# Expert blocks of a routed decoder layer: a second buffer for turned rows, a pause in queuing weight splits around turns, and one turn moved ahead of a product

## The chip, the cores and the metric

One core of a Trainium2 chip runs the whole program. The metric is the device time of one execution in microseconds (us), taken as the median of several executions; lower is better.

## The reference, cut to what matters

The layer mixes tokens (attention and a convolution), routes every token to 2 of 32 experts, and ends with a gated per-layer embedding. The change touches the experts alone:

```
def expert_block(args):               # 2048 tokens x 2 choices, grouped by expert, float32
    xb, e = args                      # xb: rows of one block of one expert, 1024 wide
    hdn = jax.nn.silu(xb @ w1[e]) * (xb @ w3[e])      # 512 wide
    return hdn @ w2[e]                                # 1024 wide
...
out = jnp.zeros((N + 1, D), ys.dtype).at[row_tok].add(ys * row_w[:, None])
```

## The kernel before

**Number format.** Every float32 factor is split into a high and a low part (`hi` is what the engine's reduced float32 keeps, `lo` the rest), and a product is made of three matmuls: hi by hi, hi by lo, lo by hi. A split is one copy on ScalarE (ACT, line 91, writes the high part) and one subtraction on VectorE (DVE, line 92, writes the low part).

**Slots and blocks.** The 32 experts are sorted by their number of tokens and put into 32 slots, 0 to 31. A slot holds one or two or three blocks. A full block has 128 rows; a small block (`few` in the code) has 64, and puts its high and low rows side by side in one operand, so that it needs two thirds of the matmuls. Slot 0 has two full blocks, slot 2 two full and one small, slots 4, 6 and 8 two full; slots 1, 3, 5, 7, 9, 11 and 13 one small; slots 10, 12, 14 and every even one to 30 a full and a small; slots 15, 17 and every odd one to 31 one full. Two blocks of a slot are worked as a pair, in turns; a single block is held over: its last products are made inside the next group.

**Weights.** A slot has 12 units of weights, each 128 x 1024 (512 KB): units 0 to 7 for the first two products, 8 to 11 for the last. "Unit 12.1" is unit 1 of slot 12 below. A unit is loaded to `eraw` (8 buffers, by SP's queue), and split to `ewh` on ACT and `ewl` on DVE (14 buffers of each).

**Steps of a block j.** X(j) turns the gathered rows by transposes on TensorE (PE, `tps<-cst,xs`) and splits them into `xt` (tag `xt` for a full block, `fx` for a small one). U(j,f,g) is a quarter of the first products (`ups`, f and g are 0 or 1; it reads units 4f+2g and 4f+2g+1); after g = 1 the block's hidden half f is made by `gated`: for a full block a SiLU on ACT and a multiplication on DVE (`hd`), for a small one a copy on ACT, an addition on DVE (`ft`), then these two. T(j,f) turns that half (`hps<-cst,hd`) and splits it into `hh`. DN(j,f,n) makes half n of the output from hidden half f (`yd`; units 8+2f and 9+2f). U of a full block is 12 matmuls of 512 columns, of a small one 8; DN 6 and 4. The transposes of X and T share two PSUM buffers (pool `et`).

**Order.** All engines run their instructions in the order in which `moe` writes them. The order of steps is written out by hand in the loop over groups. Between them the planner queues unit splits: `pe` and `dve` are clocks of its own that each step moves on, and `did`, called at the end of a step, pulls a unit as long as DVE's clock is at most 1.5 us ahead of PE's and a buffer will be free. U and DN pull what they need themselves, if it was not pulled yet, right before their own matmuls ("forced" below):

```
def U(j, f, g):
    while pulled <= 12 * j.e + 4 * f + 2 * g + 1:
        pull()
```

So the place of a split in the queues of ACT and DVE is fixed when the program is built, behind whatever was written before it, also if that waits for PE.

Of the kernel before, what the change touches and what calls it, by code (L numbers as in the profile page):

```python
# [10 lines left out]
F32R = mybir.dt.float32r  # L11
# [8 lines left out]
P = 128  # L20
# [3 lines left out]
NK = D // P  # L24
# [6 lines left out]
NE = 32  # L31
# [14 lines left out]
MOE_W = (8, 14)  # L46
# [15 lines left out]
SLACK = 1.5  # L62
# [20 lines left out]
class K:  # L83
# [808 lines left out]
    def pick(self):  # L892
# [34 lines left out]
        for g in range(4):  # L927
            nc.tensor.transpose(tp[:, g * P : (g + 1) * P], tab[:, g * P : (g + 1) * P], self.ident)
        turned = sp.tile([P, N], F32, name="turned", tag="hT")
        V.tensor_copy(turned, tp)  # L930
        dp = self.px.tile([P, N], F32, name="dps", tag="tps")
        for g in range(4):
# [39 lines left out]
    def moe(self):  # L972
# [11 lines left out]
        W, src, last = {}, [], {}  # L984
        self.last = W

        pe, dve, pulled = 0.0, 0.0, 0

        def pull():
            nonlocal pulled, dve  # L990
            e, c = pulled // 12, pulled % 12
            if c == 0:
                W[e] = []
                if e == NE:
                    src[:] = halves(A["wpp"]) + halves(A["pT"][1]) + [A["wpg"][c, i] for c in range(2) for i in range(4)]
                elif e:
                    i = nc.values_load(self.slots[0:1, 0, e : e + 1], engines=[ET.SP], min_val=0, max_val=NE - 1)
                    src[:] = [A["we"][bass.ds(i, 1), c] for c in range(12)]
                else:
                    src[:] = [A["we"][0, c] for c in range(12)]  # L1000
            W[e].append(self.unit(src[c], None, self.gathered if EARLY <= pulled < 12 else None))
            pulled += 1
            dve = max(dve, pe) + UNIT_US

        def did(us):

            nonlocal pe
            pe += us
            while dve <= pe + SLACK and pulled < 12 * NE + 12 and (pulled < MOE_W[1] or pulled - MOE_W[1] in last):
                pull()  # L1010

        def small(us):
            nonlocal dve
            dve = max(dve, pe) + us
# [9 lines left out]
        def rows(k):  # L1024
            if k < len(jobs) and jobs[k].x is None:
                j = jobs[k]
                j.x = self.xp.tile([P, D], F32, name="xs", tag="xs")[j.R]
                self.gather(col(self.idx, j.e, j.b)[j.R], j.x)

        def X(j):  # L1030
            if j is None or j.done:
                return
            j.done = True
            j.xt = self.turned(j.x, j.few)
            rows(j.k + 2)
            small(0.64 if j.few else 1.28)
            did(0.5 if j.few else 0.87)
# [4 lines that stand above are left out]
            w = W[j.e]  # L1042
            if g == 0:
                j.u[f] = self.eu.tile([P, 512], F32, name="ups", tag="eu")
            if j.few:
                self.products_few(w, j.xt, f, j.u[f], g)
            else:
                for i in range(2):
                    self.products(w, j.xt, f, j.u[f], g, i)
            if j.ends:  # L1050
                for c in range(2):
                    last[12 * j.e + 4 * f + 2 * g + c] = True
            if g == 1:
                j.h[f] = self.gated(j.u[f], j.few)
                small(1.1 if j.few else 0.4)
            did(1.82 if j.few else 2.72)

        def T(j, f):
            j.ht[f] = self.turn(j.h[f], j.few)
            small(0.4)  # L1060
            did(0.2)

        def DN(j, f, n):
            while pulled <= 12 * j.e + 8 + 2 * f + 1:
                pull()
            if f == 0:
                j.yd[n] = self.ed.tile([P, 512], F32, name="yd", tag="ed")
            self.down(W[j.e], j.yd[n], f, j.ht[f], j.few, n)
            if f and n == 0:
                j.y = self.ep.tile([P, D], F32, name="y", tag="y")  # L1070
            if f:
                yn = j.y[j.R, n * 512 : (n + 1) * 512]
                if j.few:
                    self.total(yn, j.yd[n])
                    small(0.68)
                else:
                    nc.scalar.copy(yn, j.yd[n])  # L1077
            if n and j.ends:
                for c in range(2):
                    last[12 * j.e + 8 + 2 * f + c] = True  # L1080
            did(0.91 if j.few else 1.36)
            if f and n:
                self.scatter(j.y, col(self.dst, j.e, j.b), j.R)
# [14 lines left out]
        with tc.manual_schedule(engines=set(self.engines)):  # L1098
            X(jobs[0])
            X(jobs[1])  # L1100
            for _ in range(EARLY):
                pull()
            held = []

            def release(n=1):
                for f in held[:n]:
                    f()
                del held[:n]

            for i, g in enumerate(groups):  # L1110
                nxt = groups[i + 1] if i + 1 < len(groups) else [None]
                a = g[0]
                for j in g:
                    X(j)
                U(a, 0, 0)
                release()
                if len(g) == 2:
                    b = g[1]
                    U(b, 0, 0)
                    release()  # L1120
                    U(a, 0, 1)
                    U(b, 0, 1)
                    U(a, 1, 0)
                    T(a, 0)
                    U(b, 1, 0)
                    T(b, 0)
                    U(a, 1, 1)
                    U(b, 1, 1)
                    DN(a, 0, 0)
                    T(a, 1)  # L1130
                    DN(b, 0, 0)
                    DN(a, 0, 1)
                    T(b, 1)
                    DN(a, 1, 0)
                    DN(a, 1, 1)
                    DN(b, 1, 0)
                    X(nxt[0])
                    DN(b, 0, 1)
                    DN(b, 1, 1)
                else:  # L1140

                    free = lambda j: j is not None and not (a.few and j.few)
                    if free(nxt[0]):
                        X(nxt[0])
                    U(a, 0, 1)
                    release()
                    U(a, 1, 0)
                    if not a.few:
                        T(a, 0)
                    if free(nxt[-1]):  # L1150
                        X(nxt[-1])
                    U(a, 1, 1)
                    if a.few:
                        T(a, 0)
                        held = [lambda a=a: (DN(a, 0, 0), DN(a, 0, 1), T(a, 1)), lambda a=a: (DN(a, 1, 0), DN(a, 1, 1))]
                    else:
                        DN(a, 0, 0)
                        DN(a, 0, 1)
                        held = [lambda a=a: T(a, 1), lambda a=a: (DN(a, 1, 0), DN(a, 1, 1))]
                    for j in nxt:  # L1160
                        X(j)
            release(2)
            while pulled < 12 * NE + 12:
                pull()
            self.rest()
# [70 lines left out]
    def turned(self, x, few):  # L1236

        nc = self.nc
        n, groups = (FEW, 1) if few else (P, 2)
        into = self.ep.tile([P, NK, 2 * n], F32R, name="xt", tag="fx" if few else "xt", bufs=1 if few else 2)  # L1240
        each = NK // groups
        for g in range(groups):
            ps = self.et.tile([P, 512], F32, name="tps", tag="et")
            for k in range(each):
                c = g * each + k
                nc.tensor.transpose(ps[:, k * n : (k + 1) * n], x[:, c * P : (c + 1) * P], self.ident[:n, :n])  # L1246
            s = slice(g * each, (g + 1) * each)
            self.split(into[:, s, :n], into[:, s, n:], ps.rearrange("p (k c) -> p k c", k=each))
        return into
# [211 lines left out]
```

## Time and profile before

| | us |
|---|---|
| median of 3 runs | 2820.81 (2819.8 to 2825.62) |
| the profiled execution | 2816.46 |
| its span, first to last instruction | 2814.7 |
| PE busy / weight loads / DVE / ACT / POOL | 2661.8 / 2209.8 / 1986.5 / 1471.0 / 405.6 |

The profiled execution lies 4.35 us below the median of the runs. Busy time of PE counts overlapping matmul records, so it overstates the work: matmuls of 512 columns start every 0.23 us while a record is about 0.39 us long. The expert stage runs from about 1716 to 2560 us of the span.

### The profile page before, as it was taken

Reading aid. Unit: us, or ns where it says so; the run is one execution under the profiler, and the core shown is the slowest. Engines: PE = TensorE matmul, PEld = TensorE weight load, DVE = VectorE, ACT = ScalarE, POOL = GpSimd, SP = SyncE. Lnnn points to the kernel's source line nnn. Section 1 sums busy time; section 2 is a strip of 40 time slices with the busy share of each in tenths; the row PEclk is TensorE's granted clock in tenths of the full one; section 3 lists DMA queues with packets and bytes.
Section 4 is the critical chain, followed back from the end, with each engine's and each line's share of the span. In section 5 each row is a group of like instructions: output and inputs, shape, how many; then the busy total and the mean of one; then the engine's idle time right before and its main releaser. Section 6 shows DMA issues by size and latency. Waiting matters only on the chain. (4 is left out here: it accounts for less than half of the span.)

```text
span 2814.7 us, 38600 instructions
## 1 busy us (share of the span) xinstructions
PE 2661.8 (95%) x13910; PEld 2209.8 (79%) x13911; DVE 1986.5 (71%) x3006; ACT 1471.0 (52%) x2700; POOL 405.6 (14%) x311
## 2 busy tenths in 40 slices
PE   7999999999999999989999998999999999999897
PEld 5898977898778878879789796667667777777776
DVE  6996238997787888864856746577777777775454
ACT  5232344233666666644544435566766766665333
POOL 2011122023210000000110112111111211111121
PEclk9999999999999999999999998999999999999999
DMA  5133444134433324164745637778888887885462
GB/s 191 64 113 113 139 164 150 60 124 151 164 96 103 115 76 122 37 218 150 239 161 172 210 130 270 249 281 307 294 282 301 316 316 283 314 296 182 149 209 91
DMA packets 177828, 520.83 MB, mean 185 GB/s; under 512 B 19120, under 2 KB 48576, under 8 KB 177120
## 3 DMA queue, kind: packets, MB, share of 16 engines
q1 hardware_dynamic: 135536, 397.02, 42.2%
q0 software_dynamic: 23664, 83.54, 8.0%
q10 hardware_dynamic: 18432, 37.76, 3.5%
q8 instruction: 110, 1.80, 0.3%
q14 instruction: 86, 0.70, 0.1%
HBM read 417.58 MB, written 100.66 MB: 184 GB/s over the span
## 5 line engine op out<-in xcount | busy, mean ns | idle before, releaser
L92 DVE TENSOR_TENSOR ewl<-eraw,ewh 128x1024 fp32r<-128x1024 f32 x464 | 549.5, 1219 | 140.7 <-ACT ewh L91 138.5
L91 ACT ACTIVATE ewh<-eraw 128x1024 fp32r<-128x1024 f32 x464 | 468.5, 1052 | 64.6 <-PE mps L97 27.2
L387 DVE SCALAR_TENSOR_TENSOR co<-cb,pvt,co 128x1024 f32<-128x1024 f32 x240 | 312.2, 1338 | 1.6
L96 PE MATMUL ps<-uh,wh 128*128 128x512 f32 x576 | 232.4, 406 | 4.3 <-ACT uh L91 4.3
L586 DVE TENSOR_REDUCE nm<-sc 128x1 f32<-128x512 f32 (+3 forms) x320 | 185.0, 605 | 62.0 <-PE sc L583 47.9
L97 PE MATMUL ps<-ul,wh 128*128 128x512 f32 x576 | 228.5, 398 | 0.0
L98 PE MATMUL ps<-uh,wl 128*128 128x512 f32 x576 | 227.3, 396 | 0.0
L1269 PE MATMUL ups<-ewh,xt 128*128 128x512 f32 x480 | 194.7, 406 | 5.5 <-ACT ewh L91 5.3
L1270 PE MATMUL ups<-ewl,xt 128*128 128x512 f32 x480 | 189.5, 395 | 2.1 <-DVE ewl L92 2.1
L96 PE MATMUL ps<-wh,uh 128*128 128x384 f32 x512 | 173.0, 338 | 0.0
L98 PE MATMUL ps<-wh,ul 128*128 128x384 f32 x512 | 172.1, 336 | 0.0
L97 PE MATMUL ps<-wl,uh 128*128 128x384 f32 x512 | 172.0, 336 | 0.0
L1207 POOL DMA_INDIRECT Y<-y,dst x49 | 66.4, 1355 | 657.2 <-ACT y L1077 483.1
L96 PE MATMUL mps<-ewh,mh 128*128 128x256 f32 x512 | 149.8, 293 | 3.0 <-ACT mh L91 3.0
L97 PE MATMUL mps<-ewl,mh 128*128 128x256 f32 x512 | 145.3, 284 | 0.0
L98 PE MATMUL mps<-ewh,ml 128*128 128x256 f32 x512 | 144.8, 284 | 0.0
L96 PEld LDWEIGHTS ps<-uh,wh 128*128 128x128 f32 x576 | 109.0, 190 | 32.5 <-ACT uh L91 5.0
L97 PEld LDWEIGHTS ps<-ul,wh 128*128 128x128 f32 x576 | 109.1, 189 | 28.7 <-issue 1.9
L1272 PE MATMUL ups<-ewh,xt 128*128 128x512 f32 x480 | 129.6, 392 | 0.0
L98 PEld LDWEIGHTS ps<-uh,wl 128*128 128x128 f32 x576 | 108.7, 189 | 26.3
L582 PE MATMUL sc<-Kt,Qt 128*128 128x512 f32 (+2 forms) x320 | 126.3, 401 | 3.2 <-ACT pr L572 2.8
L91 ACT ACTIVATE ah<-tp 128x512 fp32r<-128x512 f32 x144 | 82.5, 603 | 82.3 <-PE tp L632 68.5
(338 smaller groups left out, 6922.1 us busy)
## 6 DMA issues: line engine op xcount, KB each, us to landing
eraw<-in_we SPq DMA_DIRECT2D x384, 512.0 KB, 5.4
G<-sg POOLq DMA_DIRECT2D x64, 256.0 KB, 2.9
eraw<-in_wac SPq DMA_DIRECT2D x32, 512.0 KB, 4.1
ga<-G SPq DMA_DIRECT2D x32, 512.0 KB, 4.9
eraw<-in_wo SPq DMA_DIRECT2D x32, 512.0 KB, 3.7
ys<-Y SPq DMA_DIRECT2D x32, 512.0 KB, 7.2
wraw<-in_wqkv SPq DMA_DIRECT2D x16, 768.0 KB, 4.4
wraw<-in_wg SPq DMA_DIRECT2D x20, 512.0 KB, 3.9
```

Source lines behind the costliest of these rows:

```text
L91: nc.scalar.activation(hi, x, AF.Copy)
L92: (lo_eng or nc.vector).tensor_tensor(lo, x, f32(hi), ALU.subtract)
L96: nc.tensor.matmul(ps, lh, rh, start=start, stop=False)
L97: nc.tensor.matmul(ps, lh, rl, start=False, stop=False)
L98: nc.tensor.matmul(ps, ll, rh, start=False, stop=stop)
L387: nc.vector.scalar_tensor_tensor(acc, cb[:, i : i + HALF], wi, acc, ALU.mult, ALU.add)
L582: nc.tensor.matmul(sc[:, :n], Qt[:, 2 * m, qs], ks, start=True, stop=False)
L586: nc.vector.tensor_reduce(nm[:, qi, m, c : c + 1], sc[:, :w], AX.X, ALU.max, negate=True)
L1207: self.nc.gpsimd.indirect_dma_start(out=self.Y[:, :], out_offset=bass.IndirectOffsetOnAxis(ap=dst[R], axis=0), in_=y[R], in_offset=None)
L1269: self.nc.tensor.matmul(ps, xt[:, k, :P], wk[0], start=k == 0, stop=False)
L1270: self.nc.tensor.matmul(ps, xt[:, k, :P], wk[1], start=False, stop=False)
L1272: self.nc.tensor.matmul(ps, xt[:, k, P:], wk[0], start=False, stop=k == NK - 1)
```

## The change

Four edits, all in `moe` and `turned`. (1) The tile for the turned rows of small blocks has two buffers, not one, and the rule that held X of a small block back next to another small block is gone. (2) A flag `hold` stops `did` from pulling units: over U(a,0,0) of a new group and the first release of a held block, where there is one; and in a pair from U(b,1,1) to T(a,1). What U and DN need themselves is still pulled. (3) In a pair, X of the next group's block is written ahead of U(a,1,1) where that block is small, not behind DN(b,1,0). (4) The second turn T(a,1) of a held small block is released ahead of its first DN steps, not behind them.

```
-        pe, dve, pulled = 0.0, 0.0, 0
+        pe, dve, pulled, hold = 0.0, 0.0, 0, False
...
-            while dve <= pe + SLACK and pulled < 12 * NE + 12 and (pulled < MOE_W[1] or pulled - MOE_W[1] in last):
+            while not hold and dve <= pe + SLACK and pulled < 12 * NE + 12 and (pulled < MOE_W[1] or pulled - MOE_W[1] in last):
                 pull()
...
                 for j in g:
                     X(j)
+                hold = bool(held)
                 U(a, 0, 0)
                 release()
+                hold = False
                 if len(g) == 2:
...
                     T(b, 0)
+                    if nxt[0] and nxt[0].few:
+                        X(nxt[0])
                     U(a, 1, 1)
+                    hold = True
                     U(b, 1, 1)
                     DN(a, 0, 0)
                     T(a, 1)
+                    hold = False
                     DN(b, 0, 0)
...
-                    free = lambda j: j is not None and not (a.few and j.few)
-                    if free(nxt[0]):
-                        X(nxt[0])
+                    X(nxt[0])
                     U(a, 0, 1)
...
-                    if free(nxt[-1]):
-                        X(nxt[-1])
+                    X(nxt[-1])
                     U(a, 1, 1)
                     if a.few:
                         T(a, 0)
-                        held = [lambda a=a: (DN(a, 0, 0), DN(a, 0, 1), T(a, 1)), lambda a=a: (DN(a, 1, 0), DN(a, 1, 1))]
+                        held = [lambda a=a: (T(a, 1), DN(a, 0, 0), DN(a, 0, 1)), lambda a=a: (DN(a, 1, 0), DN(a, 1, 1))]
...
-        into = self.ep.tile([P, NK, 2 * n], F32R, name="xt", tag="fx" if few else "xt", bufs=1 if few else 2)
+        into = self.ep.tile([P, NK, 2 * n], F32R, name="xt", tag="fx" if few else "xt", bufs=2)
```

How the order moves, at three places. The lines of helpers move by 2 (1261 becomes 1263, and so on).

DVE at the seam of the small block of slot 11 and the pair of slot 12, before (`ft` and the first `hd` of each two are the small block's `gated`, `hh` of 64 its turns, `xt` of 64 the small block of slot 12, `y` the small block's output, the last `hd` that of slot 12's full block):

```order
L1261 TENSOR_TENSOR ft<-ft,ups 64x512
L1286 TENSOR_TENSOR hd<-hd,ft 64x256
L92 TENSOR_TENSOR hh<-hps,hh 128x2x64
L92 TENSOR_TENSOR xt<-tps,xt 128x8x64
L92 TENSOR_TENSOR ewl<-eraw,ewh 128x1024 x3
L92 TENSOR_TENSOR hh<-hps,hh 128x2x64
L92 TENSOR_TENSOR ewl<-eraw,ewh 128x1024 x2
L1261 TENSOR_TENSOR y<-y,yd 64x512 x2
L1286 TENSOR_TENSOR hd<-hd,ups 128x256
L92 TENSOR_TENSOR ewl<-eraw,ewh 128x1024 x2
```

The same place now:

```order
L1263 TENSOR_TENSOR ft<-ft,ups 64x512
L1288 TENSOR_TENSOR hd<-hd,ft 64x256
L92 TENSOR_TENSOR hh<-hps,hh 128x2x64
L92 TENSOR_TENSOR ewl<-eraw,ewh 128x1024 x5
L92 TENSOR_TENSOR hh<-hps,hh 128x2x64
L1263 TENSOR_TENSOR y<-y,yd 64x512 x2
L92 TENSOR_TENSOR ewl<-eraw,ewh 128x1024 x2
L1288 TENSOR_TENSOR hd<-hd,ups 128x256
L92 TENSOR_TENSOR ewl<-eraw,ewh 128x1024
L1263 TENSOR_TENSOR ft<-ft,ups 64x512
L1288 TENSOR_TENSOR hd<-hd,ft 64x256
L92 TENSOR_TENSOR ewl<-eraw,ewh 128x1024 x3
```

Before, the first three splits behind the first turn are units 12.3 to 12.5; now the five there are units 11.9 to 12.1, and the two behind `y` are 12.2 and 12.3, which U(a,0,1) of slot 12 reads at once.

DVE from the last quarter of a pair late in the stage (slot 30), before: the first `hd` belongs to U(a,1,1), `ft` and the second `hd` to U(b,1,1), the two `hh` to T(a,1) and T(b,1):

```order
L1286 TENSOR_TENSOR hd<-hd,ups 128x256
L92 TENSOR_TENSOR ewl<-eraw,ewh 128x1024
L1261 TENSOR_TENSOR ft<-ft,ups 64x512
L1286 TENSOR_TENSOR hd<-hd,ft 64x256
L92 TENSOR_TENSOR ewl<-eraw,ewh 128x1024 x2
L92 TENSOR_TENSOR hh<-hps,hh 128x256
L92 TENSOR_TENSOR hh<-hps,hh 128x2x64
```

And now:

```order
L1288 TENSOR_TENSOR hd<-hd,ups 128x256
L92 TENSOR_TENSOR ewl<-eraw,ewh 128x1024 x2
L1263 TENSOR_TENSOR ft<-ft,ups 64x512
L1288 TENSOR_TENSOR hd<-hd,ft 64x256
L92 TENSOR_TENSOR hh<-hps,hh 128x256
L92 TENSOR_TENSOR ewl<-eraw,ewh 128x1024 x2
L92 TENSOR_TENSOR hh<-hps,hh 128x2x64
```

The two splits that stood ahead of the full block's `hh` stand behind it.

PE at the same seam of slots 11 and 12, before: the end of U(a,0,0), then the small block's DN steps with half 0 and its turn:

```order
L1272 MATMUL ups<-ewh,xt 128x512 x4
L1254 MATMUL yd<-ewh,hh 128x512
L1255 MATMUL yd<-ewl,hh 64x512 x2
L1257 MATMUL yd<-ewh,hh 128x512
L1254 MATMUL yd<-ewh,hh 128x512
L1255 MATMUL yd<-ewl,hh 64x512 x2
L1257 MATMUL yd<-ewh,hh 128x512
L1294 MATMUL hps<-cst,hd 128x64 x2
```

And now:

```order
L1274 MATMUL ups<-ewh,xt 128x512 x4
L1296 MATMUL hps<-cst,hd 128x64 x2
L1256 MATMUL yd<-ewh,hh 128x512
L1257 MATMUL yd<-ewl,hh 64x512 x2
L1259 MATMUL yd<-ewh,hh 128x512
```

The turn stands ahead of the eight matmuls of the two DN steps.

## Rows read from the trace of the kernel before

**Rows 1.** Windows, whole expert stage and one stall: us, busy (count) per engine, clock, DMA.

```profile
core 0: us, PE busy (x) PEld busy (x) DVE busy (x) ACT busy (x) POOL busy (x), PEclk, DMA share, GB/s
1716.00:2560.00 844.00, 798.39 (x3659) 607.26 (x3659) 622.67 (x745) 565.54 (x806) 121.64 (x96) 0.98 0.84 296
...
2094.00:2098.00 4.00, 3.24 (x9) 2.32 (x10) 4.00 (x4) 2.65 (x3) 0.00 (x0) 0.69 0.92 317
```

**Rows 2.** Waits of PE in the expert stage: total us, times, longest us.

```profile
PE yd L98 <- DVE hh L92: 14.9, 23, 1.2
PE yd L96 <- ACT hh L91: 8.1, 7, 1.4
PE ups L1254 <- DVE xt L92: 5.4, 3, 3.3
PE ups L1269 <- ACT ewh L91: 5.3, 2, 3.5
```

**Rows 3.** Timeline, late pair (slot 26): start us, us, instruction, [idle before].

```profile
2428.24 1.99 ACT L91 ACTIVATE ewh<-eraw 128x1024 fp32r<-128x1024 f32 x2
...
2430.26 0.74 ACT L91 ACTIVATE hh<-hps 128x256 fp32r<-128x256 f32 x2
...
2432.07 0.50 PE L98 MATMUL yd<-ewh,hh 128*128 128x512 f32 x1 [0.64 <-DVE hh L92]
```

**Rows 4.** Timeline, PE in an early pair (slot 14).

```profile
2122.89 0.34 PE L1294 MATMUL hps<-cst,hd 64*128 64x64 f32 x2
2124.37 0.50 PE L96 MATMUL yd<-ewh,hh 128*128 128x512 f32 x1 [1.15 <-ACT hh L91]
```

**Rows 5.** Timeline, a held full block (slot 27) inside the next group.

```profile
2451.49 5.79 ACT L91 ACTIVATE ewh<-eraw 128x1024 fp32r<-128x1024 f32 x6
...
2452.57 6.90 DVE L92 TENSOR_TENSOR ewl<-eraw,ewh 128x1024 fp32r<-128x1024 f32 x6 [0.53 <-ACT ewh L91]
...
2459.39 0.41 DVE L92 TENSOR_TENSOR hh<-hps,hh 128x256 fp32r<-128x256 f32 x1
...
2459.86 0.51 PE L98 MATMUL yd<-ewh,hh 128*128 128x512 f32 x1 [0.70 <-DVE hh L92]
```

**Rows 6.** Timeline, seam of slot 13's small block and slot 14's pair.

```profile
2089.51 0.33 PE L1294 MATMUL hps<-cst,hd 64*128 64x64 f32 x2
...
2091.43 0.40 PE L1269 MATMUL ups<-ewh,xt 128*128 128x512 f32 x1
...
2091.66 0.39 PE L1270 MATMUL ups<-ewl,xt 128*128 128x512 f32 x1
...
2092.76 3.90 ACT L91 ACTIVATE ewh<-eraw 128x1024 fp32r<-128x1024 f32 x4
2092.90 0.69 DVE L92 TENSOR_TENSOR xt<-tps,xt 128x512 fp32r<-128x512 f32 x1 [0.17 <-ACT xt L91]
2093.84 4.63 DVE L92 TENSOR_TENSOR ewl<-eraw,ewh 128x1024 fp32r<-128x1024 f32 x4 [0.25 <-ACT ewh L91]
2093.86 0.50 PE L1269 MATMUL ups<-ewh,xt 128*128 128x512 f32 x1 [1.81 <-ACT ewh L91]
2095.12 0.50 PE L1270 MATMUL ups<-ewl,xt 128*128 128x512 f32 x1 [0.76 <-DVE ewl L92]
2095.46 0.56 PE L1269 MATMUL ups<-ewh,xt 128*128 128x512 f32 x1
2095.82 0.63 PE L1270 MATMUL ups<-ewl,xt 128*128 128x512 f32 x1
2096.25 1.91 PE L1272 MATMUL ups<-ewh,xt 128*128 128x512 f32 x4
```

**Rows 7.** Timeline, PE: first products of slots 9, 11, 13 and 15.

```profile
1984.85 0.39 PE L1254 MATMUL ups<-ewh,xt 128*128 128x512 f32 x1
...
2032.20 0.50 PE L1254 MATMUL ups<-ewh,xt 128*128 128x512 f32 x1 [0.52 <-DVE xt L92]
...
2081.07 0.50 PE L1254 MATMUL ups<-ewh,xt 128*128 128x512 f32 x1 [1.59 <-DVE xt L92]
...
2133.72 0.50 PE L1269 MATMUL ups<-ewh,xt 128*128 128x512 f32 x1 [0.19 <-ACT xt L91]
```

**Rows 8.** Timeline, PE at the seam of slots 5 and 6.

```profile
1894.14 0.33 PE L1294 MATMUL hps<-cst,hd 64*128 64x64 f32 x2 [0.72 <-DVE xt L92]
...
1898.19 0.50 PE L1254 MATMUL yd<-ewh,hh 128*128 128x512 f32 x1 [0.76 <-DVE hh L92]
```

More of the change, by code (lines that the diff above doesn't have):

```diff
@@ L985, in moe @@
         self.last = W
-        pe, dve, pulled = 0.0, 0.0, 0
+        pe, dve, pulled, hold = 0.0, 0.0, 0, False
         def pull():
@@ L1008, in did @@
             pe += us
-            while dve <= pe + SLACK and pulled < 12 * NE + 12 and (pulled < MOE_W[1] or pulled - MOE_W[1] in last):
+            while not hold and dve <= pe + SLACK and pulled < 12 * NE + 12 and (pulled < MOE_W[1] or pulled - MOE_W[1] in last):
                 pull()
@@ L1114, in moe @@
                     X(j)
+                hold = bool(held)
                 U(a, 0, 0)
                 release()
+                hold = False
                 if len(g) == 2:
@@ L1126, in moe @@
                     T(b, 0)
+                    if nxt[0] and nxt[0].few:
+                        X(nxt[0])
                     U(a, 1, 1)
+                    hold = True
                     U(b, 1, 1)
@@ L1130, in moe @@
                     T(a, 1)
+                    hold = False
                     DN(b, 0, 0)
@@ L1140, in moe @@
                 else:
-                    free = lambda j: j is not None and not (a.few and j.few)
-                    if free(nxt[0]):
-                        X(nxt[0])
+                    X(nxt[0])
                     U(a, 0, 1)
@@ L1149, in moe @@
                         T(a, 0)
-                    if free(nxt[-1]):
-                        X(nxt[-1])
+                    X(nxt[-1])
                     U(a, 1, 1)
@@ L1154, in moe @@
                         T(a, 0)
-                        held = [lambda a=a: (DN(a, 0, 0), DN(a, 0, 1), T(a, 1)), lambda a=a: (DN(a, 1, 0), DN(a, 1, 1))]
+                        held = [lambda a=a: (T(a, 1), DN(a, 0, 0), DN(a, 0, 1)), lambda a=a: (DN(a, 1, 0), DN(a, 1, 1))]
                     else:
@@ L1239, in turned @@
         n, groups = (FEW, 1) if few else (P, 2)
-        into = self.ep.tile([P, NK, 2 * n], F32R, name="xt", tag="fx" if few else "xt", bufs=1 if few else 2)
+        into = self.ep.tile([P, NK, 2 * n], F32R, name="xt", tag="fx" if few else "xt", bufs=2)
         each = NK // groups
```

## The prediction

> **What bounds the kernel now.** I read the busy times by window first. Over the expert stage PE works almost throughout, DVE 74% and ACT 67% of it [rows 1]: PE sets the pace, and a change in order pays only where PE waits. The table of waits then says for what: most often for the low or high half of a turned hidden half (`hh`), 23 times 0.65 us and 7 times 1.2 us, then three times for `xt`, twice for a weight's high half [rows 2]. The timeline says why `hh` is late. In a late pair ACT does two weight splits before it reaches the turn's split, though that was waiting, and PE stands 0.64 us at the matmul that needs the low half [rows 3]. In the pairs of slots 10 to 18 PE stands once more, 1.15 us for the high half [rows 4]. At a held full block six splits stand ahead of the turn, and PE waits 0.70 us [rows 5]. All these turns are late by queue order, not for lack of engine time.
>
> The seam of a small block and the next group shows the other kind of wait. A small block needs 48 matmuls, some 11 us of PE at 0.23 each [rows 6], while its slot needs 12 splits, 13.9 us of DVE at 1.16 (4.63 for four [rows 6]), besides its own additions and turns; so a small slot eats the lead that a full pair leaves. At slot 14 the lead was gone: unit 14.1 stood behind the small block's `gated`, turn and X, and PE waited 1.81 us for its high and 0.76 for its low half [rows 6]. That is the most a single missing unit showed, and the change makes more units missing.
>
> **What the change removes.** A wait costs its idle time plus about 0.27: a matmul's record lasts 0.39 to 0.40 while the next starts after 0.23, which makes 0.16 [rows 6], and the first behind a wait is 0.1 longer.
>
> - Late pairs: the two splits ahead of `hh` go behind it. `hh` moves forward by the 1.99 us of the two copies [rows 3], more than the wait, so the wait goes: 0.64 + 0.27 = 0.9 in each of the six pairs of slots 20 to 30, and 1.15 + 0.64 + 2 x 0.27 = 2.3 [rows 3, 4] in those of slots 16 and 18. Sum 10.0. What is late next is the small block's `hh`, now behind two or three splits, with 12 matmuls (2.7 us) between its turn and its use: three splits at 1.16 just miss that where they come. I put 1.0 for all of these together, between nothing and 3.
> - Held full blocks: four splits, not six, stand ahead of the turn, which frees DVE 2.3 us earlier against a wait of 0.70 [rows 5]: 0.97 in each of the seven of slots 17 to 29, 6.8.
> - Slots 0 to 4: the second buffer lets X of the small block of slot 3 go ahead of the products of slot 2's, and the longest wait for `xt`, 3.3 us [rows 2], falls away, though weight units 4.0 and 4.1, forced before and after, cost part of it again (I leave 2 of it). The first pair loses its waits for `hh`, some 2.4. With half a us at slots 1 and 4 each: 5.4.
>
> Gathers and scatters on POOL and the loads on SP keep their number; a gather is written where its X is, hence earlier or at the same place.
>
> **What it adds.** A pull that `hold` stops isn't made up for: the planner lets DVE's clock be 1.5 us ahead at most, so it pulls two units at the next step and no more. Through the slots with small blocks the lead shrinks, and U pulls what is missing itself. The order shows it: behind the small block of slots 5, 7 and 9 the second unit of the next slot (6.1, 8.1, 10.1) is forced; at slots 12 and 14 it is five units (11.9 to 12.1, 13.9 to 14.1). They stand behind the small block's `gated`, which waits for PE's last product.
>
> Price of five, slot 12. Rows 6 give the single one: PE's last product of the small block ended at 2089.51, the high half of unit 14.1 came 4.35 later (2093.86), the low half 5.6 later (2095.12). Without the `xt` split ahead of it (0.7, it moves forward) and with four units more at 1.16 the last low half comes at 5.6 - 0.7 + 4.6 = 9.5; my count along the queue from the small block's copy on gives 8.9, and I take 9.0. Seven matmuls are left then, 1.6. Undisturbed, turn and U(a,0,0) take 2.9. Loss: 7.7. It doesn't end there. Units 12.2 and 12.3 stand behind the output of the small block, which PE ends right before U(a,0,1) needs them: a copy of about 0.6 (an estimate: the `xt` split over as many columns takes 0.69 [rows 6]), a high half at 1.0 and a low one at 1.2, so some 2.9. Units 12.4 and 12.5 stand behind `gated` of the full and the small block, needed at once by U(a,1,0): about 3.0 by the same chain as rows 6. With about 1.8 for units 11.7 and 12.11: 15.4 of new waits. Of what slot 12's stretch lost before, the pair's waits with the slow matmuls behind them (3.9), the `xt` wait (1.9) and smaller ones (1.1) go. Net +8.5 on its 48.87 us [rows 7].
>
> Slot 14 has the same 15 us of new waits, but its 52.65 us [rows 7] already had 5.0 for unit 14.1, and the pair's waits of about 5 go: +5.0.
>
> Slots 9 and 10: unit 10.0 comes 1.9 late, 10.1 another 3, less what goes: +2.4 on 47.35 [rows 7]. Slots 5 and 6, 7 and 8: before, PE waited 0.72 for a PSUM buffer that X still held and 0.76 for the small block's `hh` [rows 8]. Now X's split has one unit more ahead of it (+1.15), unit 6.1 comes 2.7 late behind `gated`, and the `hh` wait is covered: +2.4 each. Slot 15: units 16.0 and 16.1 stand third and fourth behind its last `gated` with 2.7 us to go: 2.4 lost, 1.0 won by its turn, +1.4.
>
> The second turn of a held small block, moved up, needs a hidden half that is ready, by the same counts, about when it is reached; I cost it at nothing. Were it to wait at all of the seven seams it could be 1 us each, but a PE that is held there by weights hides it.
>
> **The clock.** After the wait in rows 6 matmuls start 0.43 apart (2095.82 to 2096.25) against 0.23 before it (2091.43 to 2091.66): 1.2 in place of 2.4 GHz, with a mean granted clock of 0.69 over those 4 us [rows 1]. Six to eight slow matmuls cost 1.2 to 1.6. Of these I count one for each of the five forced seams, 1.3 each, 6.5; none would be the lower bound, two each the upper. The Trainium skill, in "TensorE: Matmul & The Clock Gate" (section "HAM oscillation — how this bites in real kernels"), describes a matmul loop that waits once per iteration and is slowed again after each wait. By that rule each seam pays again at every wait, three times at slots 12 and 14: four drops more, and the sum below would be 5.2 higher. The rows show one stretch of slow matmuls behind two waits, so I stay with one per seam. Without any, the sum would be about +1.
>
> **Sum.** Gains 10.0 + 6.8 + 5.4 = 22.2. Losses 8.5 + 5.0 + 3 x 2.4 + 1.4 + 1.0 + 6.5 = 29.6. Net +7.4. On the profiled execution 2816.46 + 7.4 = 2823.9; that one lies 4.35 below the median of the runs, so I predict 2820.8 + 7.4 = 2828.
>
> **Rivals.**
> - *The late units aren't late* (faster). Over the stage DVE has a quarter of its time free [rows 1]; if the five units at slots 12 and 14 ran while PE is still in the small block's products, only the gains stay: 22.2 and the pairs' waits of slots 10 to 14 (about 12), less some 5 of small ones: 2820.8 - 29 = 2792; with half the losses true, 2807. It decides by whether unit 12.1's low half lands within 2 us behind the small block's last product. Against it: a queue in order, where even one unit landed 5.6 us after [rows 6].
> - *Gains and losses cancel* (no change): no clock drops, or the waits at U(a,0,1) and U(a,1,0) hidden by one another: 2818 to 2826.
> - *The waits for `hh` only change their place*: the small block's `hh` or U's weights take over in the late pairs too, and 10 to 17 of the gains go: 2838 to 2845. Against it: late in the stage the units pulled are again those of before, limited by the 14 buffers.
>
> **Chances and range.** A measurement of this kernel can tell about 0.2%, 5.6 us, from no change. Slower by more: 0.53 (the forecast 0.42, the third rival 0.11). Within: 0.31. Faster: 0.16. The bounds of the parts (clock 0 to 13, small waits 0 to 3, each count at slots 12 and 14 right within 3) give 2817 to 2839 for the likeliest case; with the neighbours for 8 in 10, 2810 to 2841.
>
> **What would show it.** Right: at slots 12 and 14 PE waits of 4 us and more for `ewh` at U(a,0,0), then shorter ones at U(a,0,1) and U(a,1,0); the stretch from slot 11 to 13 near 57 to 59 us; the waits for `hh` (L98 and L96) down from 23.0 to below 8; pairs from slot 16 on 2 us shorter with the single block behind them. Wrong: `ewl` of the five units lands before PE asks; or granted clock stays at full speed across the seams.

## The result and the profile after

| | before | after |
|---|---|---|
| median (4 runs each, side by side) | 2820.31 (2817.09 to 2825.62) | 2850.5 (2846.82 to 2851.15) |
| span of the profiled execution | 2814.7 | 2844.8 |
| mean granted clock over the span | 0.981 | 0.975 |

The ratio is 1.0103 [1.0085, 1.012]: the change makes the kernel 30 us (1.03%) slower. The forecast was 2828 in a range to 2841, so the direction was right and the size four times too small.

First the waits of PE over the expert stage, window 1716 to 2590 of the changed kernel (total us, times, longest us; it answers to [rows 2]; helper lines stand 2 higher than before):

```profile
PE ups L1271 <- ACT ewh L91: 25.9, 11, 5.6
PE ups L1272 <- DVE ewl L92: 12.0, 16, 1.1
PE hps L1296 <- DVE xt L92: 8.7, 4, 2.2
PE tps L1248 <- DVE hh L92: 5.4, 6, 3.7
PE yd L1259 <- DVE hh L92: 3.0, 4, 0.8
...
PE yd L98 <- DVE hh L92: 1.4, 2, 1.2
PE yd L96 <- ACT hh L91: 1.0, 1, 1.0
```

The waits for a full block's turned hidden half, which the pause was put at, fell from 14.9 + 8.1 [rows 2] to 1.4 + 1.0. In their place stand 37.9 us for weights. The timeline shows one such wait, at the seam of slots 11 and 12, all engines (start, us, instruction, [idle before]; `ft` is the small block's `gated`):

```profile
2058.94 0.33 PE L1296 MATMUL hps<-cst,hd 64*128 64x64 f32 x2
2059.04 0.58 ACT L1262 COPY ft<-ups 64x512 f32<-64x512 f32 x1 [0.93 <-PE ups L1259]
...
2060.98 4.83 ACT L91 ACTIVATE ewh<-eraw 128x1024 fp32r<-128x1024 f32 x5
2062.06 5.76 DVE L92 TENSOR_TENSOR ewl<-eraw,ewh 128x1024 fp32r<-128x1024 f32 x5 [0.63 <-ACT ewh L91]
2064.92 0.79 PE L1271 MATMUL ups<-ewh,xt 128*128 128x512 f32 x1 [5.65 <-ACT ewh L91]
2066.75 0.79 PE L1272 MATMUL ups<-ewl,xt 128*128 128x512 f32 x1 [1.03 <-DVE ewl L92]
```

ACT could not begin the five splits (units 11.9 to 12.1, fourth and fifth of them the ones PE needs) before it had done its part of the small block's `gated`, which waited for PE's last product of that block. PE then stood 5.65 us for the high half and 1.03 for the low one. That is the forced seam of the prediction. It does not end there; PE in the next quarters U(a,0,1) and U(a,1,0) of the same slot:

```profile
2078.59 0.50 PE L1271 MATMUL ups<-ewh,xt 128*128 128x512 f32 x1 [1.63 <-ACT ewh L91]
2079.88 0.63 PE L1272 MATMUL ups<-ewl,xt 128*128 128x512 f32 x1 [0.79 <-DVE ewl L92]
2080.30 0.63 PE L1271 MATMUL ups<-ewh,xt 128*128 128x512 f32 x1
...
2088.92 0.50 PE L1271 MATMUL ups<-ewh,xt 128*128 128x512 f32 x1 [1.02 <-ACT ewh L91]
2090.18 0.68 PE L1272 MATMUL ups<-ewl,xt 128*128 128x512 f32 x1 [0.76 <-DVE ewl L92]
```

Behind each of the three pairs of waits matmuls start 0.42 to 0.43 apart, not 0.23. Windows over these three stretches, between them and behind them (PEclk, third from the right, is the granted clock):

```profile
core 0: us, PE busy (x) PEld busy (x) DVE busy (x) ACT busy (x) POOL busy (x), PEclk, DMA share, GB/s
2066.00:2071.00 5.00, 4.25 (x12) 3.14 (x13) 1.83 (x2) 0.00 (x0) 0.00 (x0) 0.61 1.02 408
2071.00:2078.00 7.00, 5.96 (x26) 3.89 (x26) 1.36 (x3) 1.86 (x4) 0.00 (x0) 1.00 0.21 82
2078.00:2084.00 6.00, 4.62 (x12) 3.45 (x13) 2.68 (x3) 1.48 (x2) 0.91 (x1) 0.72 0.64 197
2084.00:2089.00 5.00, 3.37 (x15) 1.91 (x12) 2.76 (x5) 3.41 (x6) 0.00 (x0) 1.00 0.27 65
2089.00:2094.00 5.00, 4.24 (x12) 3.05 (x13) 3.40 (x3) 1.88 (x3) 0.00 (x0) 0.66 0.65 227
2094.00:2100.00 6.00, 6.00 (x34) 4.46 (x33) 2.66 (x5) 2.62 (x6) 0.89 (x1) 1.00 0.73 261
```

So the clock fell to its lower level three times in one slot and was back between. Now the slots as wholes. PE's first products of slots 9, 11 and 13 and of slot 16's small block, which answer to [rows 7]:

```profile
1996.97 0.39 PE L1256 MATMUL ups<-ewh,xt 128*128 128x512 f32 x1
...
2048.84 0.39 PE L1256 MATMUL ups<-ewh,xt 128*128 128x512 f32 x1
...
2112.01 0.39 PE L1256 MATMUL ups<-ewh,xt 128*128 128x512 f32 x1
...
2197.52 0.48 PE L1256 MATMUL ups<-ewh,xt 128*128 128x512 f32 x1
```

From slot 11 to 13 it is 63.17 us, against 48.87 before [rows 7]. Taken this way from first product to first product, the difference of the two traces falls on these stretches (us, after minus before; the forecast is the prediction's terms of that stretch, with its clock drops):

| stretch | forecast | after | pause alone | without moved X | lead lost in another way | best version |
|---|---|---|---|---|---|---|
| stage start to slot 5 | -5.4 | +3.7 | +4.0 | -0.2 | +1.5 | +1.1 |
| 5 to 9 | +7.4 | +10.5 | +0.8 | +2.3 | +2.9 | -1.0 |
| 9 to 11 | +3.7 | +4.5 | -1.2 | -1.0 | +0.8 | -1.5 |
| 11 to 13 | +9.8 | +14.3 | +17.7 | +16.8 | +4.4 | -1.5 |
| 13 to 16 (its small block) | +8.7 | +14.2 | +16.2 | +15.4 | +16.3 | -7.9 |
| 16 to 30 (their small blocks) | -14.9 | -11.9 | -11.6 | -12.0 | +2.1 | -15.3 |
| sum | +9.3 | +35.2 | +25.8 | +21.4 | +28.0 | -26.1 |

The last four columns are the experiments below called hold_only, no_x_move, starve and catch_no_x. The changed kernel reaches the stage's first product 2 us earlier and wins another 3 behind slot 30's small block; what runs ahead of the experts differs by several us between profiles of the same code, which is why stretches are taken from the stage's own first product. The profiled executions of the kernel before and after lie about 4 us below their medians, those of hold_only and no_x_move 6.7 and 5.5 above theirs, so these two columns add up to more than their medians say, and their small entries tell little.

Over the whole stage the waits of PE for weights, turned rows, turned halves and PSUM buffers add up to some 17 us more than before. Counted over every matmul of 512 columns in the stage, 110 records are longer than 0.545 us (slow ones take 0.63) instead of 51: 59 x 0.2 = 12 us. Together that is 29 of the 30 us.

### The profile page after: what moved, and what is told of

It reads as the page before. It is cut to its first block, busy times and chain, and to the rows that moved or that the text cites. A ratio compares the mean times of both kernels' runs of the same rounds, so it can differ in the third digit from the quotient of the medians.

```text
span 2844.8 us, 38623 instructions
## 1 busy us (share of the span) xinstructions
PE 2674.2 (94%) x13910; PEld 2216.3 (78%) x13911; DVE 1992.0 (70%) x3006; ACT 1468.4 (52%) x2700; POOL 402.1 (14%) x311
## 5 line engine op out<-in xcount | busy, mean ns | idle before, releaser
L1271 PE MATMUL ups<-ewh,xt 128*128 128x512 f32 x480 | 201.3, 419 | 25.9 <-ACT ewh L91 25.9
L1272 PE MATMUL ups<-ewl,xt 128*128 128x512 f32 x480 | 198.9, 414 | 12.0 <-DVE ewl L92 12.0
L1274 PE MATMUL ups<-ewh,xt 128*128 128x512 f32 x480 | 135.2, 405 | 0.0
L1271 PEld LDWEIGHTS ups<-ewh,xt 128*128 128x128 f32 x480 | 94.0, 196 | 49.7 <-ACT ewh L91 30.7
```

Source lines behind the costliest of these rows:

```text
L1271: self.nc.tensor.matmul(ps, xt[:, k, :P], wk[0], start=k == 0, stop=False)
L1272: self.nc.tensor.matmul(ps, xt[:, k, :P], wk[1], start=False, stop=False)
L1274: self.nc.tensor.matmul(ps, xt[:, k, P:], wk[0], start=False, stop=k == NK - 1)
```

## Experiments

The theory after the result was: the pause is not given back, so the planner's clocks leave PE short of units behind small blocks, and the forced splits stand behind `gated`. The rivals were that the pause harms where it stands, as a wait (the hold over U(a,0,0) above all), or that edits 1, 3 and 4 carry the loss. An expectation with several branches names them itself. Medians are compared with runs of the kernel before on the same chip: 2818.58 for no_hold, hold_only, catch_up and hold_late, 2819.88 for no_x_move, no_t_move, release_only and pair_only, 2819.22 for starve, slack4, catch_no_x and catch_only.

### Which part carries the loss

**no_hold**: the whole change without edit 2.

```
-                hold = bool(held)
+                hold = False
...
-                    hold = True
+                    hold = False
```

> The changed kernel without the pause (edit 2 undone; second buffer, moved X and moved turn stay). Theory A, the units that the pause didn't pull are late at the seams of slots 4 to 16: the seams go back to what they were, the late pairs and held blocks lose their gain of 13 again, and what is left of edits 1, 3 and 4 is small: 2816 to 2826. Rival B, the moved X and turn cause the loss through the two shared PSUM buffers and the queue order: the seams stay slow and the late gain is lost as well, 2845 to 2865.

Measured: 2823.42, ratio 1.0018 [1.0008, 1.0027], in theory A's range. Without the pause the other three edits cost 5 us, next to the bound of what a measurement can tell. Its waits of PE show why they give nothing:

```profile
PE yd L98 <- DVE hh L92: 15.1, 25, 1.2
PE tps L1248 <- DVE hh L92: 8.7, 7, 3.4
PE yd L96 <- ACT hh L91: 6.8, 6, 1.2
PE ups L1271 <- ACT ewh L91: 5.4, 2, 3.5
```

The old waits for `hh` are there, the weights' 5.4 too, and a new row (`tps`, X that waits for `hh`) takes 8.7.

**hold_only**: the kernel before, with edit 2 alone.

```
-            while dve <= pe + SLACK and ...
+            while not hold and dve <= pe + SLACK and ...
...
+                hold = bool(held)
                 U(a, 0, 0)
                 release()
+                hold = False
...
+                    hold = True
                     U(b, 1, 1)
                     DN(a, 0, 0)
                     T(a, 1)
+                    hold = False
```

> The kernel before with the pause alone (edit 2). Theory A: it has the same small lead of units at slots 6 to 16 as the changed kernel, so nearly the whole loss: 2840 to 2852. Rival B: it has the late gain without the loss, 2795 to 2810.

Measured: 2838.88, ratio 1.0066 [1.0046, 1.0086], a little under the range given. The pause alone makes some 19 of the 30 us, and in its table of waits the same row leads:

```profile
PE ups L1273 <- ACT ewh L91: 25.1, 8, 5.6
```

Its loss lies in slots 11 to 16 (the table above); at slots 5 to 9 it loses almost nothing.

**pair_only** (`hold = bool(held)` made `hold = False`: only the pause in the pair stays) and **release_only** (the pair's `hold = True` made `False`: only the pause at U(a,0,0) and the release stays):

> The changed kernel with the pause only in pairs, from U(b,1,1) to T(a,1). Lead at slots 6 to 16: 2, 4, 5, 3, 2, 5, one forced at slot 14, nearly that of the kernel before (5, 5, 5, 3, 2, 5). Theory A: the seams cost little more than before, the pairs' gain of 15 or so stays, the held blocks' 8 is lost: 2804 to 2818. Rival B: 2845 or more.

> The changed kernel with the pause only over U(a,0,0) and the release of a held block. Lead of units at the first product of slots 6, 8, 10, 12, 14, 16: 3, 4, 5, 2, 2, 2, two of them forced at slot 12 and five at slot 14 (changed kernel 2, 2, 2, 2, 2, 2, with 1, 1, 1, 5, 5 forced). Theory A: most of the 15 us of slots 5 to 11 and half of slot 12's 14 come back, slot 14's 14 stay, the pairs' gain of some 15 is lost: 2830 to 2845. Rival B (seams slow without regard to the lead): 2850 or more, since only a gain is taken away.

Measured: pair_only 2809.37, 0.9958 [0.9943, 0.9973], as expected. release_only 2850.84, 1.0108 [1.0088, 1.0128], where 2830 to 2845 was expected: a miss. This half alone is as slow as the whole change. The time alone would fit rival B; its trace does not: slots 5 to 11 lose 5.7 where the whole change loses 15.0, and slots 11 to 13 lose 6.0 where it loses 14.3, so the seams go with the lead, as theory A has it. It loses 24.4 us from the first product of slot 10 to that of slot 16's small block (before, the planner had 3 and 2 units in hand at slots 12 and 14; now 2, and both of them forced at slot 12, five at slot 14). From there to slot 30 it loses 5.7 where the change wins 11.9, more than the 15 that the expectation gave the pairs. The pause of the pair costs none of the lead that is short: five, three and two units are in hand at slots 10, 12 and 14, as before.

### Whether it is the lost lead

**catch_up**: the whole change, but the PE time that passes under the pause is lent to the planner, so that it pulls what was held back as soon as the pause ends.

```
-            dve = max(dve, pe) + UNIT_US
+            dve = max(dve, pe - back) + UNIT_US
...
             pe += us
+            back += us if hold else 0.0
             while not hold and ...
                 pull()
+            back = back if hold else 0.0
...
-            dve = max(dve, pe) + us
+            dve = max(dve, pe - back) + us
```

> The changed kernel, with the time of a pause given back to the planner: its DVE clock may lie behind by the length of the pause, so that the units that were not pulled in it are pulled right behind it. All four edits stay. The lead at the first products of slots 5 to 16 is that of the kernel before or one unit more. Theory A: the seams' 45 us go and the late gain stays: 2795 to 2812. Rival B: the seams stay slow, 2838 to 2852. Rival C, that a burst of units behind a turn makes the next turn late: late gain lost, 2815 to 2828.

Measured: 2798.6, ratio 0.9923 [0.9902, 0.9943], in theory A's range. The same pauses at the same places, and 20 us under the kernel before where the change is 30 over it. The wait of 5.65 is gone; of PE's waits for `ewh` there remains

```profile
PE ups L1273 <- ACT ewh L91: 4.1, 2, 3.5
```

So a pause is not harmful where it stands; what harms is that the units it held back were never pulled in time.

**starve**: the opposite test. The kernel before, with a pause over U(a,0,1) and U(b,0,1) of the pairs ahead of slot 16, where no turn is due, and nothing else of the change.

```
+                    hold = a.e < 16
                     U(a, 0, 1)
                     U(b, 0, 1)
+                    hold = False
```

> The kernel before with a pause where no turn is due: over U(a,0,1) and U(b,0,1) of the pairs of slots below 16. No other edit. It cuts the lead of units at slots 6, 8, 10, 12, 14 to 2, 3, 4, 2, 2, with 2 units forced at slot 12 and 5 at slot 14 (kernel before: 5, 5, 5, 3, 2 with 0 and 1 forced). Theory A, the lost lead alone makes the loss: the stretch from the first product of slot 13 to that of slot 16's small block gets some 14 us longer, as in the changed kernel, slot 12 some 3 to 6, the rest as before: 2832 to 2844. Rival, that the loss needs the pause at the turns or the moved steps: 2817 to 2824.

Measured: 2845.72, ratio 1.0092 [1.0069, 1.0115], slightly above the range. PE's waits:

```profile
PE ups L1273 <- ACT ewh L91: 17.2, 7, 5.6
PE yd L98 <- DVE hh L92: 14.5, 24, 1.2
```

The longest wait is again 5.6, while the waits for `hh` stay as before [rows 2]. Taking the lead away at another place, where no turn is due, makes a loss of that size too: by the table it falls on slot 14 above all, where five units are forced, as in the changed kernel.

**hold_late**: hold_only, with both pauses from slot 16 on only (`hold = bool(held) and a.e >= 16`, `hold = a.e >= 16`).

> The kernel before with the pause from slot 16 on alone; the other edits are left out. There the 14 weight buffers limit the pulls, and the lead is that of before within one unit. Theory A and B: the late gain alone, six pairs and seven held blocks at about 1.0 and two pairs at 2.3, less about 1.0 at each of some pairs where the small block's turned half is late: 2803 to 2812. If the gain late in the stage came from the other edits: 2818 to 2823.

Measured: 2800.74, ratio 0.9933 [0.9914, 0.9952], a little better than expected. Where no small block stands alone between the pairs, the pause costs no lead and gives its gain.

**slack4**: the change with more lead from the planner, `SLACK = 4.0` in place of 1.5.

> The changed kernel with one number changed: the planner may queue units until DVE's clock is 4.0 us ahead, not 1.5. The lead at slots 6 to 16 is 6, 7, 7, 6, 5, 10, more than in the kernel before, and nothing is forced there. Theory A: the seams are cured, 43 us come back, though turns stand behind one or two more units: 2798 to 2818. If splits ahead of the turns matter more than the lead: 2820 or more.

Measured: 2832.16, ratio 1.0046 [1.0031, 1.0061]; the first range was missed, the second branch came true. By the order of the program nothing is forced now (5 to 10 units in hand at slots 6 to 16), and of PE's waits for weights one of 0.8 is left. Others stand in their place:

```profile
PE tps L1248 <- DVE hh L92: 14.9, 6, 4.4
PE hps L1296 <- DVE xt L92: 10.5, 4, 3.1
PE hps L1296 <- DVE hd L1288: 7.1, 4, 3.0
```

Units pulled further ahead stand in front of X's and `gated`'s instructions in the same queues. Lead is not free: when it is taken matters.

### The other edits

**no_x_move**: the change without edit 3.

```
-                    if nxt[0] and nxt[0].few:
-                        X(nxt[0])
```

> The changed kernel without edit 3: X of a following small block stands behind DN(b,1,0) again. The lead of units at the seams is that of the changed kernel. Of the 12 us that edits 1, 3 and 4 cost together under the pause, theory B1 gives most to this X, which waits for the PSUM buffer of T(a,0) in the first pair (3.7 us there) and takes it from the pair's turns: 2840 to 2846. Theory B2, the turn moved up or the second buffer cost it: 2847 to 2853.

Measured: 2833.7, ratio 1.0048 [1.0031, 1.0064]: some 17 us better than the whole change, more than expected. The moved X costs in two ways. First a wait of its own; PE and DVE in the pair of slot 0 of the changed kernel:

```profile
1741.44 0.71 PE L1248 MATMUL tps<-cst,xs 64*128 64x64 f32 x8 [3.71 <-DVE hh L92]
1742.07 0.72 PE L1271 MATMUL ups<-ewh,xt 128*128 128x512 f32 x1
1742.59 0.63 PE L1272 MATMUL ups<-ewl,xt 128*128 128x512 f32 x1
...
1736.42 4.62 DVE L92 TENSOR_TENSOR ewl<-eraw,ewh 128x1024 fp32r<-128x1024 f32 x4
1740.96 0.42 DVE L92 TENSOR_TENSOR hh<-hps,hh 128x256 fp32r<-128x256 f32 x1
```

X is third in a row behind T(a,0) and T(b,0), which share two PSUM buffers with it. It needs T(a,0)'s, and the split that empties that stands behind four weight splits. PE stands 3.71 us in place of going on with U(a,1,1), and the clock falls (eight matmuls at 0.43 behind it). Second, it takes part of the lead: with it one unit is forced at each of slots 6, 8 and 10, without it none, and slots 5 to 11 lose 15.0 with it and 1.3 without it. At slot 6 (PE, end of slot 5's small block and U(a,0,0)):

```profile
1896.94 0.34 PE L1296 MATMUL hps<-cst,hd 64*128 64x64 f32 x2 [2.22 <-DVE xt L92]
...
1899.81 0.79 PE L1271 MATMUL ups<-ewh,xt 128*128 128x512 f32 x1 [1.42 <-ACT ewh L91]
1901.07 0.79 PE L1272 MATMUL ups<-ewl,xt 128*128 128x512 f32 x1 [0.47 <-DVE ewl L92]
```

The first wait was 0.72 before [rows 8]; without the moved X it is 1.67.

**no_t_move**: edit 4 undone (`held` back to DN, DN, T).

> The changed kernel without edit 4: the held small block's second turn stands behind its first DN steps again. Theory B2: 2840 to 2846. B1, the turn moved up is hidden where PE is held by weights and costs or gives nothing: 2847 to 2853.

Measured: 2854.08, ratio 1.0121 [1.0099, 1.0142], just above B1's branch. The moved turn gives about 4 us, or nothing: the two intervals overlap, and over the stretches of the table the two traces differ by 0.5 us.

**catch_no_x** and **catch_only** look for the best version. The first is catch_up without edit 3; the second is the kernel before with edit 2 and the give-back lines of catch_up, without edits 1, 3 and 4.

> The kernel that gives the pause back to the planner (2798.6 before), without edit 3: X of a following small block behind DN(b,1,0). The lead of units doesn't change by it. If edit 3's 16 us in the changed kernel came through the units that it kept back (one forced at slots 6, 8 and 10), it costs little here: 2795 to 2802. If the moved X costs by itself (its wait for a PSUM buffer), 2783 to 2793.

> The kernel before with the pause and its give-back alone, without the second buffer, the moved X and the moved turn. The lead is that of the kernel before. Theory A: nearly the whole gain of the version with all edits, whose other part is the three waits for xt (5.4 us) and the moved turn (some 4): 2800 to 2812.

Measured: catch_no_x 2787.68 (2787.0 to 2790.55), ratio 0.9889 [0.987, 0.9909], the fastest of all, 1.1% faster than before and 2.2% faster than the change. catch_only 2790.52, ratio 0.9899 [0.9879, 0.9919], better than expected. catch_no_x fell in the branch in which the moved X costs by itself. Edits 1 and 4 add some 3 us, and the two intervals overlap. The moved X costs 11 also when the lead is there (2798.6 against 2787.68); about 8 of it fall ahead of slot 5. PE's waits and first products of slots 11 and 13 in catch_no_x:

```profile
PE hps L1296 <- DVE xt L92: 6.4, 4, 3.0
PE tps L1248 <- DMA xs<-T,idx: 4.7, 4, 1.9
PE ups L1271 <- ACT ewh L91: 4.0, 2, 3.4
...
2030.68 0.49 PE L1256 MATMUL ups<-ewh,xt 128*128 128x512 f32 x1
...
2078.02 0.50 PE L1256 MATMUL ups<-ewh,xt 128*128 128x512 f32 x1 [1.12 <-DVE xt L92]
```

47.34 us from slot 11 to 13, where the change takes 63.17; five units are in hand at slots 6, 8 and 10, three and two at 12 and 14, as before, and one of the two at 14 is no longer forced.

## Why the prediction was right in direction and wrong in size

**Right.** A pause without give-back takes the lead, five units are forced at slots 12 and 14, and PE waits for them behind `gated`: catch_up, starve and hold_only show this, the timeline shows it at the places named. The price of the first wait was near: 9.1 us lost at U(a,0,0) of slot 12, slow matmuls included, against 7.7 plus one drop of 1.3. The waits for `hh` fell below 8 as said. A held full block gave 1.0 us against 0.97.

By the table the stage lost 26 us more than forecast: 9 ahead of slot 5, 14 at the five forced seams (slots 5 to 16) and 3 in the late gain.

**Wrong: the drops of the clock.** The step was "Of these I count one for each of the five forced seams, 1.3 each, 6.5". At slots 12 and 14 there are three, one behind each group of waits, and a drop takes six to eleven slow matmuls, 1.2 to 2.2 us. The five seams together have 76 slow matmuls, 15 us, more than twice the term and above its upper bound of two drops each; with what went elsewhere, the whole stage has 59 more than before. The rule that I set aside there, in the Trainium skill's "TensorE: Matmul & The Clock Gate" (section "HAM oscillation — how this bites in real kernels"), describes a loop with one long wait for a DMA in each iteration, which is slowed anew after each. The trace agrees at slot 12, where the waits are shorter: 0.61, 0.72 and 0.66 granted in its three stretches, with 1.00 between and behind them. It does not agree at every wait of this case, as the last section shows.

**Wrong: the waits at U(a,0,1) and U(a,1,0)**, put at 2.9 and 3.0. Each cost 4.6, since with each came a slow stretch; idle alone they were 1.63 + 0.79, and 0.61 + 1.02 + 0.76. Slots 11 to 13 came out at 63.17 where 57 to 59 was said. Slots 13 to 16 missed by more (14.2 against 8.7): slot 14 has the same three groups of waits. The seam of slots 15 and 16 cost 2.4, as said; the 1.0 won there by the turn of slot 15's block falls behind this stretch.

**Wrong: "Slots 0 to 4 ... 5.4".** The gain came out as a loss of 3.7. The wait of 3.3 for `xt` did go, but I had costed the X that is moved ahead at nothing: its two PSUM buffers, and what empties them, were not looked at. The first pair's waits for `hh` turned into one of 3.71 for the PSUM buffer, and 4.44 us of idle for unit 4.0 remained, against 3.50 before. X's split held the PSUM buffer longer, too: 2.22 and 2.00 us at slots 1 and 3, where it was 0.43 and 0.46. The moved X is not the whole of it: without it (no_x_move) the stretch came out at -0.2, still 5.2 short of the gain. By the order of the program the pause alone makes four units forced at slot 4 (3.10 to 4.1) where two were, and the waits at slots 1 and 3 are 1.66 and 2.00 without the moved X.

**Wrong in size: the seams of slots 5 to 9.** "+2.4 each" and one drop made 7.4; it was 10.5. The wait for X's split grew by 1.5 at slot 5 (0.72 to 2.22) where 1.15 was said; at slot 7 it was 1.09 before, not 0.72, and grew by 1.1. Each of the two seams has about ten slow matmuls, some 2.0 in place of 1.3.

**Wrong in size: the small block's `hh` in late pairs.** 1.0 was put for all; it is 1.0 in each of the four pairs of slots 16 to 22, where three splits stand ahead of it (slot 16):

```profile
2220.17 0.42 DVE L92 TENSOR_TENSOR hh<-hps,hh 128x256 fp32r<-128x256 f32 x1
2221.11 3.50 DVE L92 TENSOR_TENSOR ewl<-eraw,ewh 128x1024 fp32r<-128x1024 f32 x3 [0.52 <-ACT ewh L91]
2224.53 0.29 DVE L92 TENSOR_TENSOR hh<-hps,hh 128x128 fp32r<-128x128 f32 x1
2224.87 0.50 PE L1259 MATMUL yd<-ewh,hh 128*128 128x512 f32 x1 [0.75 <-DVE hh L92]
```

The full block's `hh` is early now, the three splits are pulled at once behind the pause, and the small block's `hh` lands 0.75 us late. From slot 24 on only two splits stand there and the wait is gone. With that the late gain is 11.9 in place of 14.9.

**The rivals.** That the late units aren't late failed by its own mark: unit 12.1's low half, the last of the five splits, was done 8.9 us behind the small block's last product (2058.94 to 2067.82), not 2; the prediction took 9.0. PE went on a little earlier, at 2066.75, with the low half of 12.0. That waits only change their place happened in four pairs, for 4 us and not for 10 to 17.

**Left open.** No run gave the moved X a PSUM buffer of its own, so its 11 us are split into wait, slow matmuls and order by the trace alone. Of the 3 us that slots 5 to 9 lost beyond the forecast about 1.3 have no row.

## What to carry to other kernels

A pause in a planner must be paid back: what a flag keeps from the queues is still needed at its old time, and the step to look at is the one right behind the next short block, not the one that the pause protects; 50 us lay between the same pauses with and without the debt. Before a step is moved ahead, list the buffers that it takes and read what stands in the queue in front of the instruction that frees each. Give every place where PE waits a slow stretch of its own in the upper bound, and don't let neighbours share one; whether it comes was not settled by the length of the waits alone.

## What the runs showed of the hardware

Waits shorter than 2 us each were enough to bring the low clock back: at slot 12, 1.63 + 0.79 us, behind some 7 us of fast matmuls, and 1.02 + 0.76 us, behind another 4 us with one wait of 0.61 in them, brought eight and seven slow matmuls. The single wait of 0.75 in slot 16 above brought none.

The length of the waits does not decide it alone. In release_only the same two waits, 1.15 us for the high and 0.64 for the low half of `hh`, stand in every pair of slots 16 to 30. Behind them seven or eight matmuls are slow at slots 16, 20, 24 and 28, and none at 18, 22, 26 and 30. Windows of 6 us from these waits on, slots 20 and 22:

```profile
2313.00:2319.00 6.00, 5.36 (x17) 3.81 (x17) 3.59 (x5) 3.20 (x6) 0.00 (x0) 0.72 0.78 268
2365.00:2371.00 6.00, 5.36 (x28) 3.96 (x27) 3.13 (x6) 3.31 (x7) 1.17 (x2) 1.00 0.75 269
```

In the kernel before, the same two waits brought slow matmuls at slots 12 and 14 and none at 10, 16 and 18. What tells these cases apart is open.

So a missing unit can cost far more than the idle time it shows: at slots 6 and 8 one unit makes 1.9 and 1.4 us of idle for the weight itself, and about ten slow matmuls, 2 us, come with it. The two seams lost 5.5 and 4.9; the longer wait for X's split is in that too.
